# Encoder layer on one core: convolution results turned, and B·C scored, one projection later

## The chip, the cores and the metric

One core of a Trainium2 chip runs the whole layer in one launch. The metric is device time in microseconds (us), the median of three runs. The core has five engines that work side by side, each through its own list of instructions in the list's order: TensorE (PE, the matrix products), VectorE (DVE), ScalarE (ACT), GpSimd (POOL) and SyncE (SP, which here only sends transfers).

## What is computed

The reference is one layer of a bidirectional hybrid encoder: 512 positions, width 1024, float32. The change lies in branch A, a Mamba-2 SSD with 4 groups of 8 heads. Cut to that branch:

```
h = rms_norm(x)
z, xbc, dt_f, dt_b, q, k, v, gates = split_cols(h @ w_in, IN_SPLITS)
xbc = jax.nn.silu(depthwise_centred_conv(xbc, conv_w, conv_b))
xs, b_in, c_in = split_cols(xbc, (SSD_INNER, SSD_GROUPS * SSD_STATE, SSD_GROUPS * SSD_STATE))
...
cb = jnp.einsum('bclgn,bcsgn->bclsg', c_c, b_c)
y_diag = jnp.einsum('bclsg,bclsgr,bcsgrp->bclgrp', cb, decay, x_c)
states = jnp.einsum('bclgn,bclgr,bclgrp->bcgrpn', b_c, to_end, x_c)
y_off = jnp.einsum('bclgn,bcgrpn,bclgr->bclgrp', c_c, h_in, jnp.exp(a_cum).astype(dtype))
```

Forward and backward scans are added, gated with silu(z), normalised per group and projected back. Windowed attention, cross attention and a feed-forward part follow; they are not touched.

## The kernel before, in words

**Tiles.** The activations stand with their 1024 features in 8 slabs of 128 partitions by 512 positions. A weight tile `raw` (128 x 1024) is loaded by SP, split into a high part `whi` by ACT (L130) and a low part `wlo` by DVE (L131). One *projection* is 24 matmuls of 512 columns, three for each of 8 slabs (L140, L141, L142), into one of three PSUM banks named `mm`. A bank comes free when its last reader is through, and the projection three further on waits for that.

**A group.** For each of the 4 groups `group_in(g)` makes six projections: B, C and x0 to x3. `conv` then smooths each along the positions: ACT reads the bank (L412), DVE adds four shifted copies (L415, the last of which frees the bank), ACT takes a tanh into `cvt` (L417), DVE joins it to the result `bf`, `cf` or `xs` (L418). Three kinds of steps read these results on PE: `b_turn` transposes B (L433, four transposes, then a copy to `bt` on ACT, L434), `c_turn` multiplies B and C (L449, four matmuls, copy to `cb` on ACT, L450), and `x_turn(i)` transposes x(i) (L471, copy to `xk` on ACT, L472). Each step stands in the program behind a later projection, so that PE has that one to work on while the convolution is finished by DVE and ACT.

**What uses them.** `group_scan` has a list per head: SP loads rows of decay `rt` (three buffers), POOL masks them (`head`, L538, two selects a head), ACT takes eight exponentials (L545), POOL adds both directions into `mt` (L551, which also frees the `rt` buffer for the head three further on), DVE multiplies by `cb` (`times`, L556), PE multiplies with `xk` (`inner`, L566). `weigh` (POOL, L496) and `carry` (PE L504, DVE L509 and L511) build the states `hin`, `arrive` (PE, L578) applies them, `gather` (DVE and POOL, L586 to L591) adds up `vv`, `gate` (L603) multiplies with z. `group_out` (L645 for the first group, then L648 on DVE and L649 on POOL with a single buffer `cvt`) projects the group before. In group 0 its place is taken by projections of the cross attention's keys (`xw`, L262 on DVE).

**What sets the order.** Everything up to about 540 us stands in one block, `tc.block(schedule_with_timeline_sim=True)`. A scheduler, not the source, decides in which order each engine there gets its instructions; the source order is what it starts from. The lists it makes are fixed at build time: each engine then runs its own in that order. Behind the block the source order holds.

Of the kernel before, what the change touches and what calls it, by code (L numbers as in the profile page):

```python
# [55 lines left out]
ZP = 2  # L56
# [10 lines left out]
def weave(a, b):  # L67

    key = [((i + 0.5) / len(a), 0, i) for i in range(len(a))] + [((i + 0.5) / len(b), 1, i) for i in range(len(b))]
    return [(a, b)[w][i] for _, w, i in sorted(key)]  # L70
# [3 lines left out]
def bidir_hybrid_layer(ctx: ExitStack, tc: tile.TileContext, io, dbg=None):  # L74
# [20 lines left out]
    def bank(tag):  # L95
        return ps.tile([P, 512], F32, tag=tag, name=tag, bufs={"mm": 3, "sa": 2, "sb": 3}[tag])
# [99 lines left out]
    steps = []  # L196
# [7 lines left out]
    def full(src):  # L204
        return (src, 1024)
# [201 lines left out]
    def conv(w, ct, dst):  # L407
        sp, hcw = st["sp"], st["hcw"]
        acc = proj(w, st["hh"], st["hl"])
        u = sp.tile([P, S], F32, tag="cvu", name="cvu", bufs=2)  # L410
        w5 = [hcw[:, 5 * ct + j:5 * ct + j + 1] for j in range(5)]
        nc.scalar.activation(u, acc, AF.Identity, bias=hcw[:, 120 + ct:121 + ct], scale=w5[2])  # L412
        for j, a, b in ((0, slice(0, S - 2), slice(2, S)), (1, slice(0, S - 1), slice(1, S)),
                        (3, slice(1, S), slice(0, S - 1)), (4, slice(2, S), slice(0, S - 2))):
            nc.vector.scalar_tensor_tensor(u[:, b], acc[:, a], w5[j], u[:, b], op0=ALU.mult, op1=ALU.add)  # L415
        th = sp.tile([P, S], F32, tag="cvt", name="cvt", bufs=1)
        nc.scalar.activation(th, u, AF.Tanh)  # L417
        nc.vector.scalar_tensor_tensor(dst, th, 1.0, u, op0=ALU.add, op1=ALU.mult)  # L418

    def group_in(g):  # L420
        gb = G_SSD + 10 * g

        def b_step(w):
            sp = st["sp"]
            bf = sp.tile([P, S], F32, tag="bf", name="bf")
            conv(w, 16 + g, bf)
            st["bf", g] = bf

        def b_turn():
            bt = st["sp"].tile([P, S], F32, tag="bt", name="bt")  # L430
            tp = bank("sb")
            for c in range(NCH):
                nc.tensor.transpose(tp[:, c * P:(c + 1) * P], st["bf", g][:, c * P:(c + 1) * P], ident)  # L433
            nc.scalar.copy(bt, tp)  # L434
            st["bt", g] = bt

        def c_step(w):
            sp = st["sp"]
            cf = sp.tile([P, S], F32, tag="cf", name="cf", bufs=2)
            conv(w, 20 + g, cf)  # L440
            b_turn()
            st["cf", g] = cf

        def c_turn():
            cb = st["sp"].tile([P, S], F32, tag="cb", name="cb", bufs=2)
            tp = bank("sb")
            for c in range(NCH):
                c_ = slice(c * P, (c + 1) * P)
                nc.tensor.matmul(tp[:, c_], st["bf", g][:, c_], st["cf", g][:, c_], start=True, stop=True)  # L449
            nc.scalar.copy(cb, tp)  # L450
            st["cb", g] = cb

        def x_step(i):
            def f(w):
                sp = st["sp"]
                if i == 0:
                    st["xk", g] = sp.tile([P, NCH, S], F32, tag="xk", name="xk", bufs=2)
                xs = sp.tile([P, S], F32, tag="xs", name="xs", bufs=XSB)
                conv(w, 4 * g + i, xs)
                st["xs", g, i] = xs  # L460
                if i == 0:
                    c_turn()
                else:
                    x_turn(i - 1)()
            return f

        def x_turn(i):
            def f():
                tp = bank("sb")
                for c in range(NCH):  # L470
                    nc.tensor.transpose(tp[:, c * P:(c + 1) * P], st["xs", g, i][:, c * P:(c + 1) * P], ident)  # L471
                nc.scalar.copy(st["xk", g][:, :, i * P:(i + 1) * P], tp.rearrange("p (c l) -> p c l", c=NCH))  # L472
            return f

        w = io["w_in"]
        return ([(b_step, (full(w[gb]),)), (c_step, (full(w[gb + 1]),))]
                + [(x_step(i), (full(w[gb + 2 + i]),)) for i in range(4)], [(x_turn(3), ())])

    def group_z(g):
        def z_step(i):  # L480
            def f(w):
                acc = proj(w, st["hh"], st["hl"])
                zs = st["sp"].tile([P, S], F32, tag="zs", name="zs", bufs=4)
                nc.scalar.activation(zs, acc, AF.Tanh, scale=0.5)
                nc.vector.scalar_tensor_tensor(zs, zs, 1.0, acc, op0=ALU.add, op1=ALU.mult)
                st["zs", g, i] = zs
            return f
        return [(z_step(i), (full(io["w_in"][G_SSD + 10 * g + 6 + i]),)) for i in range(4)]
# [148 lines left out]
    def group_out(g):  # L637
        def f2(q):
            def f(w):
                for j in range(2):  # L640
                    m = 2 * q + j
                    acc = bank("mm")
                    mac(acc, w, st["vh"], st["vl"], nk=4, w0=4 * j)
                    if g == 0:
                        nc.vector.tensor_tensor(bs[:, m], acc, st["vrow"], op=ALU.mult)  # L645
                    else:
                        t = st["sp"].tile([P, S], F32, tag="cvt", name="cvt", bufs=1)
                        nc.vector.tensor_tensor(t, acc, st["vrow"], op=ALU.mult)  # L648
                        nc.gpsimd.tensor_tensor(bs[:, m], bs[:, m], t, op=ALU.add)  # L649
            return f  # L650
        return [(f2(q), (full(io["w_bs"][g, q]),)) for q in range(4)]


    def early_gate(m):
        def f(w):
            if m == 0:
                st["eg"] = st["sp"].tile([P, NCH, S], F32, tag="xk", name="xk", bufs=2)
            acc = proj(w, st["hh"], st["hl"])
            nc.scalar.activation(st["eg"][:, m], acc, AF.Tanh, scale=0.5)
        return f  # L660
# [10 lines left out]

    add(ssd_open)
    first, last = group_in(0)
    add(dt_step, full(io["w_in"][G_DT]))
    steps += weave(first, kv[KV0:KV1])
    for g in range(G):
        z, (more, turn) = group_z(g), group_in(g + 1) if g + 1 < G else ([], [])
        scan1, scan2 = group_scan(g)
        out = group_out(g - 1) if g else kv[KV1:]
        early = [(early_gate(m), (full(io["w_in"][G_GS + m]),)) for m in range(4)] if g == G - 1 else []  # L680
        kinds = {"m": list(more), "z": z[ZP:], "o": list(out), "e": early,
                 "r": [(group_rms, ())] if g else [], "w": [(group_row, ())] if g else []}

        def take(order):
            return [kinds[c].pop(0) for c in order if kinds[c]]

        one = take(ONE if g < G - 1 else ONE + "e")
        if g == 0:
            one += take("o" * len(kinds["o"]))
        two = take(TWO if g < G - 1 else LAST)  # L690
        steps += z[:ZP] + last
        steps += weave(scan1, one)
        steps += weave(scan2, two)
        last = turn
# [442 lines left out]
    for i, (fn, gr) in enumerate(steps):  # L1137
# [5 lines left out]
        w = ready[taken:taken + len(gr)]  # L1143
# [98 lines left out]
```

## Time and profile before

| quantity | value |
|---|---|
| median of 3 runs | 1304.64 us (1303.63 to 1304.96) |
| the profiled execution | 1304.59 us |
| its span, first to last instruction | 1302.8 us |
| outside the span | 1.8 us |
| PE busy | 1253.3 us |
| DVE, ACT, POOL busy | 770.9, 565.7, 314.8 us |

The profiled execution differs from the median by 0.05 us, so that its rows can be added and taken away as they stand. Times in the rows are counted from the start of the span. A bracket behind a row gives the idle time of the engine ahead of it and what ended it. PEclk is the share of full speed that TensorE's clock was granted: 1.0 is 2.4 GHz, 0.5 is 1.2 GHz.

### The profile page before, as it was taken

Reading aid. Unit: us, or ns where it says so; the run is one execution under the profiler, and the core shown is the slowest. Engines: PE = TensorE matmul, PEld = TensorE weight load, DVE = VectorE, ACT = ScalarE, POOL = GpSimd, SP = SyncE. Lnnn points to the kernel's source line nnn. Section 1 sums busy time; section 2 is a strip of 40 time slices with the busy share of each in tenths; the row PEclk is TensorE's granted clock in tenths of the full one; section 3 lists DMA queues with packets and bytes.
Section 4 is the critical chain, followed back from the end, with each engine's and each line's share of the span. In section 5 each row is a group of like instructions: output and inputs, shape, how many; then the busy total and the mean of one; then the engine's idle time right before and its main releaser. Section 6 shows DMA issues by size and latency. Waiting matters only on the chain.

```text
span 1302.8 us, 16247 instructions
## 1 busy us (share of the span) xinstructions
PE 1253.3 (96%) x6076; PEld 1015.5 (78%) x6076; DVE 770.9 (59%) x1226; ACT 565.7 (43%) x1062; POOL 314.8 (24%) x259
## 2 busy tenths in 40 slices
PE   7898999999989999999999999999999999999996
PEld 5677787778778688877667888887888888888886
DVE  6693987687787865678874345675444444432323
ACT  6456655365465232358783234444332222222220
POOL 2343742432671733211000002001111111110001
PEclk9899999999999999999999999999999999999998
DMA  7337563444354232331104233311322222233331
GB/s 267 121 112 196 158 202 113 130 146 140 105 157 133 81 116 79 120 97 33 49 29 139 95 104 108 125 65 65 97 90 98 95 96 98 95 93 101 93 98 65
DMA packets 49614, 143.48 MB, mean 110 GB/s; under 512 B 5120, under 2 KB 8576, under 8 KB 49536
## 3 DMA queue, kind: packets, MB, share of 16 engines
q1 hardware_dynamic: 47536, 138.58, 34.4%
q0 software_dynamic: 704, 2.10, 0.4%
q10 hardware_dynamic: 1296, 1.77, 0.4%
q8 instruction: 48, 0.79, 0.3%
q14 instruction: 30, 0.25, 0.1%
HBM read 137.97 MB, written 4.46 MB: 109 GB/s over the span
## 4 chain that ended last, share of the span: by engine, by line
PE 59%; issue 5%; DVE 2%; ACT 2%; POOL 1%; DVEq 0%; ACTq 0%; POOLq 0%
PE mm L140 18%; PE mm L141 18%; PE mm L142 18%; PE sb L824 1%; PE sb L811 1%; PE sb L998 1%; PE sa L967 1%; POOL rsw L723 1%; PE sa L783 1%; ACT rsw L722 0%; PE sa L785 0%; ACT whi L130 0%; ACT sm L796 0%; PE sb L155 0%; PE sb L173 0%
## 5 line engine op out<-in xcount | busy, mean ns | idle before, releaser
L130 ACT CAST whi<-raw 128x1024 fp32r<-128x1024 f32 (+2 forms) x192 | 198.8, 1036 | 457.5 <-PE mm L141 392.0
L140 PE MATMUL mm<-hh,whi 128*128 128x512 f32 x968 | 381.8, 395 | 8.1 <-ACT hh L316 4.7
L141 PE MATMUL mm<-hl,whi 128*128 128x512 f32 x968 | 381.0, 394 | 0.8 <-DVE hl L317 0.8
L142 PE MATMUL mm<-hh,wlo 128*128 128x512 f32 x968 | 381.0, 394 | 0.0
L131 DVE TENSOR_TENSOR wlo<-raw,whi 128x1024 fp32r<-128x1024 f32 (+2 forms) x193 | 238.1, 1234 | 143.6 <-ACT whi L130 134.2
L140 PEld LDWEIGHTS mm<-hh,whi 128*128 128x128 f32 x968 | 182.3, 189 | 47.9 <-ACT hh L316 4.9
L142 PEld LDWEIGHTS mm<-hh,wlo 128*128 128x128 f32 x968 | 182.6, 189 | 38.8 <-issue 2.2
L141 PEld LDWEIGHTS mm<-hl,whi 128*128 128x128 f32 x968 | 182.6, 189 | 37.6 <-issue 1.2
L545 ACT ACTIVATE rt<-rt,nb 128x128 f32<-128x128 f32 x256 | 78.6, 390 | 58.5 <-POOL rt L538 58.4
L188 POOL TENSOR_TENSOR sq_acc<-sq_acc,sq 128x512 f32<-128x512 f32 x14 | 24.4, 1741 | 261.0 <-ACT sq L187 261.0
L1051 POOL TENSOR_TENSOR fa<-fa,row 128x512 f32<-128x512 f32 x22 | 38.8, 1762 | 192.7 <-ACT fa L1050 192.7
L140 PE MATMUL mm<-vh,whi 128*128 128x512 f32 (+1 forms) x192 | 71.9, 375 | 6.9 <-DVE cvu L415 2.7
L415 DVE SCALAR_TENSOR_TENSOR cvu<-mm,hcw,cvu 128x510 f32<-128x510 f32 (+1 forms) x96 | 71.3, 743 | 7.0 <-ACT cvu L412 5.5
L140 PE MATMUL mm<-fh,whi 128*128 128x512 f32 (+1 forms) x198 | 72.7, 367 | 0.0
L141 PE MATMUL mm<-fl,whi 128*128 128x512 f32 (+1 forms) x198 | 72.4, 366 | 0.0
L142 PE MATMUL mm<-fh,wlo 128*128 128x512 f32 (+1 forms) x198 | 72.4, 366 | 0.0
L142 PE MATMUL mm<-vh,wlo 128*128 128x512 f32 (+1 forms) x192 | 71.8, 374 | 0.0
L141 PE MATMUL mm<-vl,whi 128*128 128x512 f32 (+1 forms) x192 | 70.3, 366 | 0.0
L538 POOL TENSOR_SCALAR_AFFINE_SELECT rt<-rt 128x512 f32<-128x512 f32 x64 | 49.7, 802 | 59.1 <-DMA rt<-adr 58.9
L1053 DVE TENSOR_TENSOR ft<-fa,mm 128x512 f32<-128x512 f32 x22 | 15.1, 688 | 73.6 <-PE mm L142 71.4
L551 POOL TENSOR_TENSOR mt<-rt 128x512 f32<-128x512 f32 x32 | 45.6, 1436 | 19.6 <-PE sa L566 19.5
L141 PE MATMUL mm<-ol,whi 128*128 128x512 f32 x128 | 50.0, 391 | 0.0
(231 smaller groups left out, 1963.5 us busy)
## 6 DMA issues: line engine op xcount, KB each, us to landing
raw<-in_w_in SPq DMA_DIRECT2D x69, 512.0 KB, 3.5
raw<-in_w_fi SPq DMA_DIRECT2D x44, 512.0 KB, 3.4
rt<-adr SPq DMA_DIRECT2D x32, 512.0 KB, 5.5
ear<-edr SPq DMA_DIRECT2D x32, 256.0 KB, 4.4
raw<-in_w_bs SPq DMA_DIRECT2D x16, 512.0 KB, 3.5
raw<-in_w_fo SPq DMA_DIRECT2D x16, 512.0 KB, 3.6
raw<-in_w_xk SPq DMA_DIRECT2D x8, 512.0 KB, 3.9
raw<-in_w_ba SPq DMA_DIRECT2D x8, 512.0 KB, 3.4
```

The lines of the kernel that those rows point to most:

```text
L130: nc.scalar.copy(hi[:, t], raw[:, t])
L131: (nc.gpsimd if i in LO_POOL else nc.vector).tensor_tensor(lo[:, t], raw[:, t], hi[:, t].bitcast(F32), op=ALU.subtract)
L140: nc.tensor.matmul(acc, wh, xh[:, k0 + k], start=first and k == 0, stop=False)
L141: nc.tensor.matmul(acc, wh, xl[:, k0 + k], start=False, stop=False)
L142: nc.tensor.matmul(acc, wl, xh[:, k0 + k], start=False, stop=last and k == nk - 1)
L188: eng.tensor_tensor(acc, acc, sq, op=ALU.add)
L415: nc.vector.scalar_tensor_tensor(u[:, b], acc[:, a], w5[j], u[:, b], op0=ALU.mult, op1=ALU.add)
L538: nc.gpsimd.affine_select(out=rt[:, d].rearrange("p (c l) -> p c l", c=NCH), in_=rt[:, d].rearrange("p (c l) -> p c l", c=NCH), pattern=[[ ...
L545: nc.scalar.activation(r, r, AF.Exp, bias=st["nb"][:, c, e0:e0 + 1])
L551: nc.gpsimd.tensor_tensor(mt, st["rt", g, h][:, 0], st["rt", g, h][:, 1], op=ALU.add)
L1051: nc.gpsimd.tensor_tensor(a, a, st["row2"], op=ALU.mult)
L1053: nc.vector.tensor_tensor(t, a, st["fp", 2 * j + 1], op=ALU.mult)
```

## The change

`b_turn` leaves `c_step` and stands behind x0's projection; `c_turn` moves from x0's to x1's; `x_turn(i)` from behind x(i+1) to behind x(i+2). So x2 and x3 are still to be turned when the six projections of a group are through: `x_turn(2)` now stands behind the first of the group's z projections and `x_turn(3)` behind the second, where `x_turn(3)` alone stood behind both.

```
         def c_step(w):
...
             conv(w, 20 + g, cf)
-            b_turn()
             st["cf", g] = cf
...
                 if i == 0:
+                    b_turn()
+                if i == 1:
                     c_turn()
-                else:
-                    x_turn(i - 1)()
+                elif i > 1:
+                    x_turn(i - 2)()
             return f
...
-                + [(x_step(i), (full(w[gb + 2 + i]),)) for i in range(4)], [(x_turn(3), ())])
+                + [(x_step(i), (full(w[gb + 2 + i]),)) for i in range(4)], [(x_turn(2), ()), (x_turn(3), ())])
...
-        steps += z[:ZP] + last
+        steps += z[:1] + last[:1] + z[1:ZP] + last[1:]
```

No instruction is added or left out. Since the scheduler starts from another list, the order within the block moves on every engine, for steps too that the diff doesn't name. Line numbers behind L460 are one higher in the changed kernel (L471 is L472 there), and the number behind a name counts tiles, so that the same tile can have another number.

**DVE, group 0, where x3 (`xs`, L418) is joined.** L556 is the product of a head's `mt` with `cb`, L131 a weight's low part, L485 a z projection. Before:

```order
L131 TENSOR_TENSOR wlo_919<-raw_916,whi_918 128x1024
L485 SCALAR_TENSOR_TENSOR zs_913<-zs_913,mm_888 128x512
L556 TENSOR_TENSOR mt_1213<-mt_1213,cb_666 128x512
L418 SCALAR_TENSOR_TENSOR xs_841<-cvt_873,cvu_867 128x512
L131 TENSOR_TENSOR wlo_965<-raw_962,whi_964 128x1024
```

and changed:

```order
L131 TENSOR_TENSOR wlo_919<-raw_916,whi_918 128x1024
L486 SCALAR_TENSOR_TENSOR zs_907<-zs_907,mm_882 128x512
L557 TENSOR_TENSOR mt_1206<-mt_1206,cb_741 128x512
L418 SCALAR_TENSOR_TENSOR xs_835<-cvt_867,cvu_861 128x512
L131 TENSOR_TENSOR wlo_965<-raw_962,whi_964 128x1024
```

Here nothing moved: x3's L418 stands behind the same product.

**DVE, between group 0 and group 1**, where L262 reads the keys' projection `mm_1023` and so frees the bank for x0 of group 1. `hin` are the states (L509, L511), `vv` is the sum that `gather` starts (L586). Before:

```order
L509 TENSOR_TENSOR hin0_1063<-hin0_1053,dec_174 128x512
L415 SCALAR_TENSOR_TENSOR cvu_1131<-mm_1106,hcw_414,cvu_1131 128x511
L262 TENSOR_TENSOR xw_1048<-mm_1023,sq_263 128x256
L131 TENSOR_TENSOR wlo_1234<-raw_1231,whi_1233 128x1024
L509 TENSOR_TENSOR hin1_1068<-hin1_1058,dec_174 128x512
L586 SCALAR_TENSOR_TENSOR vv_1472<-xs_713,vec_76,sa_1418 128x512
L511 TENSOR_TENSOR hin0_1063<-hin0_1063,sb_1061 128x512
```

and changed:

```order
L510 TENSOR_TENSOR hin0_1063<-hin0_1053,dec_174 128x512
L415 SCALAR_TENSOR_TENSOR cvu_1131<-mm_1106,hcw_414,cvu_1131 128x511
L587 SCALAR_TENSOR_TENSOR vv_1465<-xs_706,vec_76,sa_1411 128x512
L131 TENSOR_TENSOR wlo_1227<-raw_1224,whi_1226 128x1024
L510 TENSOR_TENSOR hin1_1068<-hin1_1058,dec_174 128x512
L262 TENSOR_TENSOR xw_1048<-mm_1023,sq_263 128x256
L512 TENSOR_TENSOR hin0_1063<-hin0_1063,sb_1061 128x512
```

The same L262 moved behind `vv`, a weight's low part and one L509.

**ACT, between group 2 and group 3**, where L417 takes the tanh for x0 of group 3. The `rt` rows are the exponentials of group 3's heads 1, 2 and 3. Before:

```order
L417 ACTIVATE cvt_3093<-cvu_3087 128x512
L130 CAST whi_3187<-raw_3185 128x1024
L545 ACTIVATE rt_3654<-rt_3654,nb_172 128x128 x8
L545 ACTIVATE rt_3666<-rt_3666,nb_172 128x128 x8
L187 ACTIVATE sq_3395<-vv_3224 128x512
```

and changed:

```order
L449 COPY cb_3271<-sb_3272 128x512
L546 ACTIVATE rt_3654<-rt_3654,nb_172 128x128 x8
L130 CAST whi_3180<-raw_3178 128x1024
L417 ACTIVATE cvt_3086<-cvu_3080 128x512
L546 ACTIVATE rt_3666<-rt_3666,nb_172 128x128 x8
```

The tanh and the weight's high part moved from ahead of head 2's exponentials to behind them.

**POOL, at the same place.** L649 adds a tile of the group before's output to `x1` and frees `cvt`; `rt_3680` is the row of head 4, `rt_3654` that of head 2. Before:

```order
L538 AFFINE_SELECT rt_3666<-rt_3666 128x512 x2
L591 TENSOR_TENSOR vv_3224<-vv_3224,ear_2971 128x384
L551 TENSOR_TENSOR mt_3730<-rt_3652 128x512
L649 TENSOR_TENSOR x1_69<-x1_69,cvt_3144 128x512
L649 TENSOR_TENSOR x1_69<-x1_69,cvt_3160 128x512
L188 TENSOR_TENSOR sq_acc_3232<-sq_acc_3232,sq_3395 128x512
L649 TENSOR_TENSOR x1_69<-x1_69,cvt_3204 128x512
L538 AFFINE_SELECT rt_3680<-rt_3680 128x512 x2
L551 TENSOR_TENSOR mt_3748<-rt_3654 128x512
```

and changed:

```order
L539 AFFINE_SELECT rt_3666<-rt_3666 128x512 x2
L552 TENSOR_TENSOR mt_3730<-rt_3652 128x512
L552 TENSOR_TENSOR mt_3748<-rt_3654 128x512
L539 AFFINE_SELECT rt_3680<-rt_3680 128x512 x2
L650 TENSOR_TENSOR x1_69<-x1_69,cvt_3137 128x512
L539 AFFINE_SELECT rt_3736<-rt_3736 128x512 x2
L650 TENSOR_TENSOR x1_69<-x1_69,cvt_3153 128x512
```

The adds of the output tiles moved from ahead of the selects of head 4 to behind them.

## Rows read from the trace of the kernel before

**Rows 1.** First part of the page: busy time, share, instructions of each engine

```profile
PE 1253.3 (96%) x6076; PEld 1015.5 (78%) x6076; DVE 770.9 (59%) x1226; ACT 565.7 (43%) x1062; POOL 314.8 (24%) x259
```

**Rows 2.** Waits of PE, 60 to 580 us: waiter, releaser, total us, times, longest

```profile
PE sb L471 <- DVE xs L418: 5.6, 3, 4.0
...
PE sa L382 <- DVE x L375: 2.4, 1, 2.4
```

**Rows 3.** Timeline of PE, 120 to 128 us: start, duration, instruction, idle ahead

```profile
122.44 0.63 PE L471 MATMUL sb<-cst,xs 128*128 128x128 f32 x4 [4.03 <-DVE xs L418]
```

**Rows 4.** Timeline of POOL, 104 to 124 us

```profile
118.08 1.22 POOL L538 TENSOR_SCALAR_AFFINE_SELECT rt<-rt 128x512 f32<-128x512 f32 x2 [5.77 <-DMA rt<-adr]
119.26 1.26 POOL L551 TENSOR_TENSOR mt<-rt 128x512 f32<-128x512 f32 x1
```

**Rows 5.** Timeline of DVE, 104 to 124 us

```profile
121.17 1.12 DVE L418 SCALAR_TENSOR_TENSOR xs<-cvt,cvu 128x512 f32<-128x512 f32 x1
```

**Rows 6.** Timeline of PE, 143 to 151 us

```profile
148.60 0.50 PE L140 MATMUL mm<-hh,whi 128*128 128x512 f32 x1 [1.30 <-DVE xw L262]
```

**Rows 7.** Timeline of DVE, 143 to 152 us

```profile
148.14 0.41 DVE L262 TENSOR_TENSOR xw<-mm,sq 128x256 f32<-128x256 f32 x1
148.47 1.67 DVE L131 TENSOR_TENSOR wlo<-raw,whi 128x1024 fp32r<-128x1024 f32 x1
...
151.75 0.67 DVE L511 TENSOR_TENSOR hin<-hin,sb 128x512 f32<-128x512 f32 x1
```

**Rows 8.** Timeline of PE around 188, 262 and 399 us

```profile
188.22 0.66 PE L471 MATMUL sb<-cst,xs 128*128 128x128 f32 x4 [1.00 <-DVE xs L418]
...
262.50 0.47 PE L140 MATMUL mm<-vh,whi 128*128 128x512 f32 x1 [1.83 <-DVE x L645]
...
399.36 0.63 PE L471 MATMUL sb<-cst,xs 128*128 128x128 f32 x4 [0.62 <-DVE xs L418]
```

**Rows 9.** Timeline of PE, 368 to 381 us

```profile
370.42 0.47 PE L140 MATMUL mm<-vh,whi 128*128 128x512 f32 x1 [2.68 <-DVE cvu L415]
...
373.27 0.60 PE L471 MATMUL sb<-cst,xs 128*128 128x128 f32 x4
...
376.92 1.05 PE L578 MATMUL sb<-cf,hin 128*128 128x128 f32 x8
...
379.63 0.50 PE L140 MATMUL mm<-hh,whi 128*128 128x512 f32 x1 [1.29 <-DVE cvt L648]
```

**Rows 10.** Timeline of ACT, 365 to 381 us

```profile
370.39 0.64 ACT L417 ACTIVATE cvt<-cvu 128x512 f32<-128x512 f32 x1 [4.26 <-DVE cvu L415]
370.93 1.04 ACT L130 CAST whi<-raw 128x1024 fp32r<-128x1024 f32 x1
371.87 4.79 ACT L545 ACTIVATE rt<-rt,nb 128x128 f32<-128x128 f32 x16
```

**Rows 11.** Timeline of DVE, 365 to 381 us

```profile
371.06 0.73 DVE L418 SCALAR_TENSOR_TENSOR xs<-cvt,cvu 128x512 f32<-128x512 f32 x1 [0.32 <-ACT cvt L417]
...
377.21 1.77 DVE L556 TENSOR_TENSOR mt<-mt,cb 128x512 f32<-128x512 f32 x1
378.90 0.68 DVE L648 TENSOR_TENSOR cvt<-mm,vrow 128x512 f32<-128x512 f32 x1
```

**Rows 12.** Timeline of POOL, 365 to 390 us

```profile
370.61 3.87 POOL L538 TENSOR_SCALAR_AFFINE_SELECT rt<-rt 128x512 f32<-128x512 f32 x4 [2.67 <-DMA rt<-adr]
...
379.65 1.30 POOL L649 TENSOR_TENSOR x<-x,cvt 128x512 f32<-128x512 f32 x1 [1.23 <-DVE cvt L648]
...
384.07 2.00 POOL L538 TENSOR_SCALAR_AFFINE_SELECT rt<-rt 128x512 f32<-128x512 f32 x2 [0.61 <-DMA rt<-adr]
```

**Rows 13.** Timeline of SP, 365 to 381 us: when a transfer is sent

```profile
377.62 0.37 SPq L519 DMA_DIRECT2D rt<-adr  x1
```

**Rows 14.** Windows: us, busy of PE, PEld, DVE, ACT, POOL, PEclk, DMA share, GB/s

```profile
123.60:127.00 3.40, 3.40 (x16) 3.21 (x15) 1.79 (x2) 2.06 (x5) 0.59 (x2) 0.50 0.70 213
...
370.00:374.00 4.00, 3.58 (x19) 3.05 (x20) 3.67 (x6) 3.61 (x10) 3.39 (x4) 1.00 0.22 86
```

## The prediction

> **What bounds the kernel now.** I read the page's first part, then PE's waits, then the timeline of PE at each of them, then the timelines of the engines that end them, beside the new order. PE is busy 1253.3 of 1302.8 us [rows 1], so about 50 us are idle, and the change can only touch the idle time that lies in the scheduled block. There the steps that it moves are waited for three times: L471 waits 5.6 us for DVE's L418, 4.0 of it once [rows 2]. That is the prize. What DVE, ACT and POOL do in between is not busy time that counts: they set the end only where PE stands idle for them.
>
> **The 4.03 us at 122.44 us stay.** This is the largest wait of a moved step, x3 of group 0 [rows 3]. It ends when DVE has done L418, started at 121.17 [rows 5]. The order on DVE shows that L418 stands behind a head's product L556, which needs POOL's L551, done at 120.52, which needs POOL's select at 118.08, and POOL had stood idle 5.77 us there for the transfer of the head's row [rows 4]. In the changed order the same product stands ahead of the same L418, and the transposes on PE are one matmul later. To come free of this wait, the transposes would have to be behind about 4 us more of PE's work, and they are not. Value: 0, bounds 0 and -4.03.
>
> **Where it gives.** In group 1, x0 and x1 are turned two projections later on PE: the 1.00 us at 188.22 goes; in group 3, x1's transposes move from 51.5 projections after the start of the block to 53, and the 0.62 us at 399.36 goes [rows 8]. Sum -1.6, bounds 0 and -1.6 (if what they waited for is late too). The 1.83 us at 262.50 [rows 8] ends with L645 of group 0's output, not with a moved step; I leave it. A moved step itself costs what it cost: four PE instructions and one ACT copy, no transfer.
>
> **Where it takes, first place, 148.60 us.** x0's projection of group 1 waits 1.30 us for L262 [rows 6], which DVE starts at 148.14 and finishes 0.05 us ahead of PE's start [rows 7]: no slack. In the new order three instructions that stood behind L262 stand ahead of it: L586, L131, L509. In the trace these three take from 148.47 to 151.75, 3.28 us [rows 7]. PE has two matmuls of `arrive` more to do meanwhile: L578 takes 1.05 us for eight such records, four matmuls [rows 9], hence about 0.5 us. So 3.28 - 0.5 = 2.8 us at the most; 0 if DVE, whose list there is also lighter further up, has run ahead. I take 2.0, nearer to the full price, since DVE's rows leave no gap in that stretch.
>
> **Second place, 370 to 380 us.** Before, ACT takes x0's tanh at 370.39 and a cast at 370.93, and only then 16 exponentials, 4.79 us [rows 10]; DVE joins x0 at 371.06 [rows 11] and PE turns it at 373.27 without a wait [rows 9]. In the new order the first eight exponentials and the cast stand ahead of the tanh, and the place of x0's transposes on PE is the same. The exponentials need POOL's select, which waited for a transfer until 370.61 [rows 12]; they can't be earlier than 371.87 unless the row is sent earlier, and the row's buffer is freed by an L551 that now stands behind an L649 (1.30 us [rows 12]).
> The least: 371.87 + 2.40 (half of 4.79) + 0.94 (from 370.93 to 371.87) = 375.2 for the tanh, 0.67 later (as from 370.39 to 371.06) DVE's L418 at 375.9, done at 376.6: PE turns x0 3.3 us later than at 373.27.
> The chain in full: the L649 in front makes the select 1.30 later, 371.9. DVE's new order has head 1's product (L556, 1.77 us [rows 11]) ahead of L418, and it needs an L551 that stands behind all four selects: 371.9 + 3.87 + 1.26 (L551 [rows 4]) = 377.0, + 1.77 + 0.73 = 379.5 for x0. Then POOL: L649 of the output's tiles stands behind head 4's select, where before it was done ahead of it. That select waits for a row sent at 377.62 [rows 13] and started at 384.07 [rows 12]; its buffer is freed by the L551 just computed, at about the same time, 377.0. So 384.07 + 2.00 (two selects) + 1.30 (L649) = 387.4, + 0.68 (L648 [rows 11]) = 388.1 for the bank that PE had at 379.63 [rows 9]. That is 8.5 us later. PE meanwhile does work that before came later: six matmuls of L578, by the row above some 1.5 us. Net 7.0.
> The bounds are 3.3 - 1.5 = 1.8 (only the tanh is late) and 7.0. I take 6.0, near the upper, since each instruction of the chain is named in the order and has a duration from a row. The waits that stand there now (2.68 and 1.29 [rows 9]) are inside these clock times and not counted again. What is late next is the chain of group 3's heads, which hangs on these same rows and so moves along.
>
> **The clock.** After the 4.03 us idle, TensorE ran 3.4 us at 0.50 [rows 14], the lower of its two levels, 1.2 GHz: it did in 3.4 us what takes 1.7 at 2.4 GHz. Such a fall follows three idles of PE in this stretch, of 2.4 us (L382 [rows 2]), 4.03 [rows 3] and 1.83 us [rows 8], three stretches of the same kind of which one row stands here; the 2.68 us at 370.42 was followed by full clock [rows 9, 14], and so was the 1.30 at 148.60. So an idle of 2 to 4 us costs 0 or 1.7 us more, and 3 of 5 rows say 1.7. New idles of that size: at 148.60 (1.30 + 2.0 = 3.3 us), ahead of x0's transposes and ahead of the output's bank (some 3 us each), and one more as the chain recovers. I take 1.0 for the first (3/5 of 1.7) and 2.6 for the others (one and a half falls); bounds 0 and 1.7, 0 and 5.1.
> The Trainium skill, "TensorE: Matmul & The Clock Gate", section "HAM oscillation — how this bites in real kernels", tells of a kernel whose clock fell to half in every wait between its bursts. Here the 2.68 us wait speaks against "every". [...]
>
> **The sum**, against the profiled execution of 1304.59 us (span 1302.8 and 1.8 around it; 0.05 under the median, so no correction): -1.6 + 2.0 + 1.0 + 6.0 + 2.6 = +10.0, hence 1314.6 us.
>
> **The rivals.**
> *Faster: the moved steps find their data.* If x3 of group 0 is no longer waited for, because POOL's select there starts earlier than at 118.08 (SP's list of rows changes too), the three waits of L471 go, 5.6 us, and with the longest the fall behind it, 1.7: 1304.6 - 7.3 = 1297.3. For it speaks that the moves are aimed at the right waits; against it that POOL's and DVE's order there is the same. It decides where that select ends over 4 us earlier, and none of the new waits may come. Chance 0.12.
> *Slower by more: every new wait brings the clock down.* The same places, with four falls: 1.7 + 5.1 in place of 1.0 + 2.6, so +13.2, 1317.8. For it: the falls after idles as short as 1.83 and 2.4; against it the 2.68. Chance 0.20.
> *No change: the new waits are absorbed.* DVE has run ahead at 148.60 (0), only the tanh is late at 373 (1.8), no fall, -1.6 gained: +0.2, 1304.8. For it: the heads' rows, not the moved steps, pace these stretches before and after, and the lists are the same in most places. Also in here is that the change hardly does what it says, since on PE the transposes of x0 in group 3 and of x3 in group 0 keep their places. Chance 0.15.
>
> **How the numbers follow.** The forecast has 0.53, the rivals 0.12, 0.20 and 0.15. Its own range is 1309 to 1317.5. The ends of all terms: -1.6 + 0 + 0 + 1.8 + 0 = +0.2 and -1.6 + 2.8 + 1.7 + 7.0 + 5.1 = +15.0, that is 1304.8 and 1319.6. From 1303 to 1320 all but the faster rival and the tails lie inside, so some 0.85. Within 0.2% is within 2.6 us, about what a measurement of this kernel can tell from no change. Faster 0.12, same 0.15, slower 0.53 + 0.20 = 0.73.
>
> **What would show it right or wrong.** Right: PE's waits list L262 with some 3 to 4 us and an L471 ahead of which PE idles 3 us or more near 375 us; the projection that started at 379.63 starts at 385 to 389; ACT shows eight L545 ahead of that tanh; PE's idle at 122 us is still about 4 us; the waits at 188 and 399 are gone. Wrong: PE busy from 370 to 390 with waits no longer than now, or the idle at 122 gone. It would also be wrong if a stretch that I left at nothing (240 to 300, 430 to 515 us) moved by over 2 us, since the order there hardly differs and I took its waits to move along.

## The result and the profile after

The changed kernel takes 1316.06 us (median of three runs) against 1304.8 us for the kernel before, run beside it. The ratio is 1.0089 with a 95% interval of 1.0068 to 1.0109, so it is slower by about 11.6 us (8.9 to 14.2). A fourth run, 1565.85 us at a mean granted clock of 0.75, was disturbed and stands outside these figures; with it the median is 1317.44 us. The profiled execution took 1318.83 us, its span is 1317.1 us: 14.3 us more than the span of before.

The first part of the page of the changed kernel (busy time, share and instructions of each engine) answers to [rows 1]:

```profile
PE 1259.1 (96%) x6076; PEld 1018.3 (77%) x6076; DVE 769.4 (58%) x1226; ACT 565.2 (43%) x1062; POOL 313.9 (24%) x259
```

The same 6076 matmuls keep PE busy for 5.8 us more (1259.1 against 1253.3), and PE is idle for 58.0 us of the span where it was 49.5, 8.5 us more. Equal work that takes longer is the clock (its mean is 0.983 where it was 0.989); the idle time is waits. So two fifths of the 14.3 us are clock, three fifths idle time. Part of that idle time lies at the start of this execution, ahead of any difference between the kernels. Counted from 60 us on (60 to 515 us of before, 63 to 529 of the changed kernel, the same work), PE's busy time grows from 432.5 to 438.7 us and its idle time from 22.3 to 27.4: 6.2 us of clock and 5.1 of waits. The waits of PE from 60 to 600 us in the changed kernel (waiter, releaser, total us, times, longest), which answer to [rows 2]:

```profile
PE sb L472 <- DVE xs L418: 6.4, 2, 3.4
PE mm L140 <- DVE cvu L415: 5.2, 4, 2.8
PE sa L567 <- DVE mt L557: 4.7, 5, 3.0
PE sb L579 <- ACT bt L434: 2.7, 1, 2.7
PE mm L140 <- DVE cvt L649: 2.5, 4, 1.4
```

The step that the change turns later (L472, L471 before) is waited for longer than before, 6.4 us for 5.6. L567's wait for the heads' products grows from 2.8 to 4.7 us and that for `cvu`, a convolution's sum, from 3.3 to 5.2. L579's wait for `bt`, the turned B, is new, and the wait for L262 that the prediction expected isn't there.

**Where the time went.** I set the same matmul of both traces side by side and took the difference of the starts. Counted by the time of before, the changed kernel is later by 2.9 us at 60, 2.2 at 138, 10.6 at 152, 7.9 at 190, 8.7 at 345, 15.8 at 380, 14.1 at 410, and 14.2 from there to the end. So 2.9 us are there before the lists of the two kernels differ at all, which begins near 100 us: that part is how this one execution started. The change's own share is 14.2 - 2.9 = 11.3 us, close to the 11.6 above. It gains 0.7 us up to 138, loses 6.4 in the first place (138 to 345, with the 1.00 us recovered at 188 in it) and 5.5 in the second (345 to 515).

These shares are those of one execution. Set beside the trace of before in the same way, other traces with the same lists there lose 3.1 to 5.7 us in the first place (experiments 1, 6 and 7 below) and 5.4 to 7.4 in the second (experiments 2 to 5). And experiment 2, which still has the lists of before there, is 1.9 us slower from 138 to 300. So a share read from one trace is good to about 2 us.

**First place.** PE's timeline in the changed kernel, 121 to 165 us (start, duration, instruction, idle ahead and what ended it), which answers to [rows 3] and [rows 6]:

```profile
124.80 0.63 PE L472 MATMUL sb<-cst,xs 128*128 128x128 f32 x4 [3.39 <-DVE xs L418]
...
130.48 0.50 PE L140 MATMUL mm<-hh,whi 128*128 128x512 f32 x1 [1.26 <-DVE zs L486]
...
147.66 1.97 PE L567 MATMUL sa<-mt,xk 128*64 128x128 f32 x14 [2.96 <-DVE mt L557]
...
157.21 1.22 PE L579 MATMUL sb<-cf,hin 128*128 128x128 f32 x4 [2.70 <-ACT bt L434]
158.08 0.77 PE L140 MATMUL mm<-hh,whi 128*128 128x512 f32 x1
```

The projection that waited for L262 in [rows 6] follows at 158.08 without a wait. DVE had finished L262 4 us earlier, in the changed kernel:

```profile
153.64 0.41 DVE L262 TENSOR_TENSOR xw<-mm,sq 128x256 f32<-128x256 f32 x1
```

What is late is `bt`. Followed backwards on ACT and POOL of the changed kernel (the same columns):

```profile
154.24 2.45 ACT L546 ACTIVATE rt<-rt,nb 128x128 f32<-128x128 f32 x8 [8.58 <-POOL rt L539]
156.60 0.56 ACT L434 COPY bt<-sb 128x512 f32<-128x512 f32 x1
```

```profile
151.86 2.94 POOL L539 TENSOR_SCALAR_AFFINE_SELECT rt<-rt 128x512 f32<-128x512 f32 x2 [6.06 <-DMA rt<-adr]
```

ACT copies `bt` behind eight exponentials, these wait 8.58 us for POOL's select, and that one 6.06 us for the transfer of a head's row `rt`. In the kernel before the same select waited 0.81 us for its row:

```profile
144.08 1.67 POOL L538 TENSOR_SCALAR_AFFINE_SELECT rt<-rt 128x512 f32<-128x512 f32 x2 [0.81 <-DMA rt<-adr]
```

SP's timeline shows why. First the kernel before, then the changed one, 130 to 150 us (start, time on SP, instruction; the third `raw<-in_w_xk` is the last of a set of three weight loads):

```profile
132.23 2.31 SPq L122 DMA_DIRECT2D raw<-in_w_xk  x2
138.18 0.38 SPq L519 DMA_DIRECT2D rt<-adr  x1
142.40 0.33 SPq L122 DMA_DIRECT2D raw<-in_w_xk  x1
```

```profile
135.56 9.69 SPq L122 DMA_DIRECT2D raw<-in_w_xk  x3
145.31 0.94 SPq L520 DMA_DIRECT2D rt<-adr  x2
```

Before, the row goes out at 138.18 and the third weight at 142.40. After, the third weight stands ahead of the row. It can't be sent before a `raw` buffer is free: from 130 to 150 us SP's weight loads wait 17.5 us in all for DVE's L131, which reads these buffers, against 10.0 before. SP sends in the order of its list, and so the row goes out at 145.31, 7.1 us later; 2.2 of these are the lateness that this execution already had at 138.

**Second place.** The changed kernel, 380 to 397 us. On POOL, then ACT, then DVE, then PE (the same columns; they answer to [rows 9 to 12], at times that are 8.7 us later from the first place on):

```profile
380.89 1.22 POOL L539 TENSOR_SCALAR_AFFINE_SELECT rt<-rt 128x512 f32<-128x512 f32 x2 [0.72 <-DMA rt<-adr]
383.51 1.22 POOL L539 TENSOR_SCALAR_AFFINE_SELECT rt<-rt 128x512 f32<-128x512 f32 x2 [1.40 <-DMA rt<-adr]
...
391.44 1.22 POOL L539 TENSOR_SCALAR_AFFINE_SELECT rt<-rt 128x512 f32<-128x512 f32 x2 [3.25 <-DMA rt<-adr]
```

```profile
381.56 2.45 ACT L546 ACTIVATE rt<-rt,nb 128x128 f32<-128x128 f32 x8 [5.34 <-POOL rt L539]
383.91 1.03 ACT L130 CAST whi<-raw 128x1024 fp32r<-128x1024 f32 x1
384.85 0.63 ACT L417 ACTIVATE cvt<-cvu 128x512 f32<-128x512 f32 x1
```

```profile
384.98 2.08 DVE L131 TENSOR_TENSOR wlo<-raw,whi 128x1024 fp32r<-128x1024 f32 x1 [2.88 <-ACT whi L130]
386.98 1.75 DVE L557 TENSOR_TENSOR mt<-mt,cb 128x512 f32<-128x512 f32 x1
388.66 0.68 DVE L418 SCALAR_TENSOR_TENSOR xs<-cvt,cvu 128x512 f32<-128x512 f32 x1
...
393.96 0.69 DVE L649 TENSOR_TENSOR cvt<-mm,vrow 128x512 f32<-128x512 f32 x1 [0.41 <-POOL x L650]
```

```profile
381.78 0.47 PE L140 MATMUL mm<-vh,whi 128*128 128x512 f32 x1 [2.83 <-DVE cvu L415]
...
389.39 1.12 PE L472 MATMUL sb<-cst,xs 128*128 128x128 f32 x4 [3.03 <-DVE xs L418]
...
395.52 0.39 PE L140 MATMUL mm<-hh,whi 128*128 128x512 f32 x1
```

This is the chain of the prediction: select, eight exponentials, cast, tanh, with the product L557 ahead of L418 on DVE. One link in it is not in the prediction: a weight's low part, L131, also stands ahead on DVE and waits 2.88 us for the cast behind the exponentials. PE waits 3.03 us for x0, which it had at once in [rows 9]. The output's bank, freed by the L649 at 393.96, is not waited for: the projection behind it starts at 395.52 without a gap.

**The clock.** Windows of the changed kernel behind these idles (us, busy of PE, PEld, DVE, ACT, POOL, PEclk, DMA share, GB/s), which answer to [rows 14]:

```profile
123.60:127.00 3.40, 2.20 (x15) 2.06 (x16) 1.05 (x2) 2.21 (x9) 1.46 (x2) 1.00 0.57 112
147.70:151.10 3.40, 3.40 (x16) 2.02 (x16) 3.40 (x6) 0.00 (x0) 0.00 (x0) 0.50 0.99 198
157.20:160.40 3.20, 3.19 (x10) 2.71 (x11) 1.92 (x4) 2.83 (x9) 2.24 (x3) 0.50 0.81 186
382.00:386.00 4.00, 4.00 (x12) 3.06 (x11) 1.12 (x2) 4.00 (x12) 2.60 (x5) 0.57 0.09 33
389.40:392.80 3.40, 3.40 (x17) 3.40 (x18) 1.70 (x3) 1.28 (x4) 1.36 (x3) 0.52 0.97 333
```

Of these five idles of PE of 2.7 to 3.4 us, four are followed by the lower level, 1.2 GHz; the longest, 3.39 us ahead of 124.80, is followed by 2.4 GHz.

What follows an idle differs from execution to execution. The wait of 2.83 us for `cvu` ahead of 381.78 stands in eight traces, those of the changed kernel and of experiments 2 to 7 and 9. In the 4 us behind it the granted clock is 0.50 to 0.63 in five of them and 1.00 in three (experiments 4, 6 and 9). The 2.96 us ahead of 147.66 are not even the change's own: experiment 2, with the lists of before there, waits 2.92 us at that matmul, and the full clock follows.

### The profile page after: what moved, and what is told of

The parts are those of the page before. It is cut to its first block, busy times and chain, and to the rows that moved or that the text cites. A ratio compares the mean times of both kernels' runs of the same rounds, so it can differ in the third digit from the quotient of the medians.

```text
span 1317.1 us, 16255 instructions
## 1 busy us (share of the span) xinstructions
PE 1259.1 (96%) x6076; PEld 1018.3 (77%) x6076; DVE 769.4 (58%) x1226; ACT 565.2 (43%) x1062; POOL 313.9 (24%) x259
## 4 chain that ended last, share of the span: by engine, by line
PE 74%; issue 7%; DMA 6%; DVE 5%; ACT 3%; POOL 3%; SPq 0%; POOLq 0%; ACTq 0%; DVEq 0%
PE mm L140 22%; PE mm L141 22%; PE mm L142 22%; DMA rt<-adr 4%; PE sb L825 1%; PE sb L579 1%; PE sb L812 1%; PE sb L505 1%; DVE wlo L131 1%; POOL rsw L724 1%; PE sb L999 1%; ACT whi L130 1%; ACT rt L546 1%; PE sa L968 1%; POOL rt L539 1%
## 5 line engine op out<-in xcount | busy, mean ns | idle before, releaser
L131 DVE TENSOR_TENSOR wlo<-raw,whi 128x1024 fp32r<-128x1024 f32 (+2 forms) x193 | 241.6, 1252 | 164.5 <-ACT whi L130 153.9
L539 POOL TENSOR_SCALAR_AFFINE_SELECT rt<-rt 128x512 f32<-128x512 f32 x64 | 46.6, 751 | 71.3 <-DMA rt<-adr 71.3
L140 PEld LDWEIGHTS mm<-vh,whi 128*128 128x128 f32 x192 | 37.2, 194 | 17.2 <-issue 5.1
```

Of the source, the lines that this page charges most:

```text
L131: (nc.gpsimd if i in LO_POOL else nc.vector).tensor_tensor(lo[:, t], raw[:, t], hi[:, t].bitcast(F32), op=ALU.subtract)
L140: nc.tensor.matmul(acc, wh, xh[:, k0 + k], start=first and k == 0, stop=False)
L539: nc.gpsimd.affine_select(out=rt[:, d].rearrange("p (c l) -> p c l", c=NCH), in_=rt[:, d].rearrange("p (c l) -> p c l", c=NCH), pattern=[[ ...
```

## The experiments

All of them need the lists held fast, since any edit of the source makes the scheduler draw new ones. So a table `ORDER` of instruction numbers is written into the kernel, one row an engine, and each instruction is tied to the one ahead of it in its row. This ties the order alone and adds no wait, and with the kernel's own numbers it gives the kernel's own lists. An experiment then exchanges entries.

```
+def pin(tc, nc):
+    at = {x.name: x for x in nc.cur_bb.bb.instructions}
+    for row in ORDER:
+        for a, b in zip(row, row[1:]):
+            tc.add_manual_dep(at[f"I-{b}"], f"I-{a}",
...
         if i == cutat:
+            pin(tc, nc)
             blk.close()
```

The table shifts the line numbers by 16 to 20: L579 is L596 or L599 there, L472 is L489 or L492, L262 is L279, L418 is L435 or L436.

**1 and 2: one part of the change each.** `LATE` names the groups whose turns stand later. For their part of the block the table has the lists of the changed kernel, for the rest those of the kernel before. Group 2's turns stand as before in both; in the changed kernel the stretch from 190 to 300 us, where they lie, loses nothing (7.9 us late, then 7.8).

```
+LATE = (0, 1)
...
+                if g not in LATE:
+                    (c_turn if i == 0 else x_turn(i - 1))()
...
+                else:
+                    (c_turn if i == 1 else x_turn(i - 2))()
```

> Only groups 0 and 1 have the later turns; a table of instruction numbers pins each engine's list in the block: as in the changed kernel up to the start of group 2, as in the kernel before from there on. Theory A (two separate losses, one between groups 0 and 1, one between groups 2 and 3, that add up): slower than before by 4 to 7 us, about 1310 us, with PE idle some 3 us ahead of L567 and some 2.7 us ahead of L579 between 147 and 158 us, and the waits of 370 and 379 us as before. Rival B (a delay early on is absorbed later, the loss is made at group 3): within 2 us of before.

> Only group 3 has the later turns; the lists are pinned as in the kernel before up to the middle of group 2 and as in the changed kernel from there on. Theory A: slower than before by 4 to 7 us, about 1310 us, with x0's transposes of group 3 waited for some 3 us. Rival B (the loss between groups 2 and 3 comes from being late already): within 2 us of before.

Groups 0 and 1 alone: 1308.97 us, ratio 1.0023 (1.0007 to 1.0038). Group 3 alone (`LATE = (3,)`): 1312.0 us, 1.005 (1.0031 to 1.0068). Against 1305.25 for before that is +3.7 and +6.75 (by the ratios 3.0 and 6.5), together 10.5, where the whole change costs 11.6. The first is a little less than expected. Each loss is there without the other, and within their intervals they add up: two places, neither the consequence of the other. PE of the first kernel shows the first place, with `bt`, and longer than in the whole change and than expected (5.55 us for 2.70):

```profile
154.22 1.22 PE L599 MATMUL sb<-cf,hin 128*128 128x128 f32 x4 [5.55 <-ACT bt L452]
```

**3, 4, 5: undo the exchange on SP, the one on DVE, both.** In the changed kernel's table, on SP:

```
-raw<-in_w_xk x3, rt<-adr x3
+raw<-in_w_xk x2, rt<-adr, raw<-in_w_xk, rt<-adr x2
```

and on DVE:

```
-L587 vv, L131 wlo, L510 hin, L262 xw
+L262 xw, L587 vv, L131 wlo, L510 hin
```

> The changed kernel, every list pinned as it is, with one exchange on SP: the row of head 6 of group 0 (rt) is sent ahead of one weight load (raw) instead of behind it, as it was before the change. Theory A (SP's queue makes the loss between groups 0 and 1: the row waits behind a load whose buffer is not free): 4 to 6 us faster than the changed kernel, about 1311 to 1312 us; the 2.7 us wait of L579 for bt goes. Rival B (the prediction's: L262 behind three more instructions on DVE): no change, 1316 to 1317 us.

> The changed kernel, every list pinned as it is, with L262 on DVE put back ahead of the three instructions (L587, L131, L510) that the change put in front of it. Rival B (the prediction's step): 2 to 4 us faster than the changed kernel. Theory A: no change, 1316 to 1317 us, since L262 is done in time for PE there.

> The changed kernel, pinned, with both exchanges at the first place: head 6's row sent ahead of the weight load (SP) and L262 ahead of the three instructions (DVE). With the row alone exchanged, PE still waited 2.0 us for L262. Theory A' (two limits one behind the other: the row first, L262 next): 1.5 to 3 us faster than with the row alone, so some 6 us faster than the changed kernel, 1310 to 1311.5 us, and no wait over 1.5 us for L262 or bt around 150 us. Rival (L262 is a limit of its own that never decides): as with the row alone, 1313 us.

Gains over the changed kernel are taken from the ratios. The row alone: 1313.17 us (1.0055, 1.0038 to 1.0072), some 4 us less than the changed kernel. L262 alone: 1317.15 us (1.0092, 1.0064 to 1.0119), no gain; its four runs lie between 1312.62 and 1319.01 us, so that one of 2 or 3 us could hide in them. Its trace says why none is to be expected: PE still waits for `bt`, and not for L262.

```profile
150.40 0.71 PE L596 MATMUL sb<-cf,hin 128*128 128x128 f32 x4 [3.35 <-ACT bt L451]
```

Both: 1311.38 us (1.0041, 1.0024 to 1.0059), 6 us less. PE with the row alone restored, 148 to 154 us:

```profile
149.56 0.71 PE L596 MATMUL sb<-cf,hin 128*128 128x128 f32 x4 [0.68 <-ACT bt L451]
152.27 0.50 PE L157 MATMUL mm<-hh,whi 128*128 128x512 f32 x1 [2.00 <-DVE xw L279]
```

With the row back in its place the wait for `bt` falls from 2.70 to 0.68 us, and L262 (L279 here), which had been hidden by it, is now waited for 2.00 us in all; the prediction had 1.30 + 2.0 = 3.3. With both restored that wait is gone too, and set beside the trace of before the kernel is 1.0 us late at 138 and 1.2 at 345: in this trace the first place costs next to nothing. The step from the row alone to both, 1.8 us by the ratios, is within the noise; it is the wait that vanishes which shows L262 as the second limit.

**6 and 7: the second place.** First on ACT alone, then on ACT, DVE (`xs` ahead of the product, a weight's low part and a sum) and POOL (two L650 ahead of the selects of head 4):

```
-rt x8, whi, cvt, rt x8
+cvt, whi, rt x16
```

```
-ear, wlo, mt, xs, mt
+xs, ear, wlo, mt x2
...
-AFFINE_SELECT x2, x, AFFINE_SELECT x2, x x3
+x x2, AFFINE_SELECT x4, x x2
```

> The changed kernel, pinned, with one exchange on ACT between groups 2 and 3: the cast of a weight's high part and x0's tanh stand ahead of head 2's eight exponentials, as before the change. Theory C (a chain on three engines: DVE's list has x0's L418 behind a head's product that needs POOL): under 1.5 us faster than the changed kernel, 1315 to 1317 us, and L472 still waited for over 2 us near 389 us. Rival (the tanh's place on ACT is the loss, the lower bound of the prediction): 2 to 4 us faster, 1312 to 1314 us.

> The changed kernel, pinned, with the order of three engines put back between groups 2 and 3: on ACT cast and tanh ahead of head 2's exponentials, on DVE x0's L418 right behind its last shifted copy, on POOL two adds of output tiles ahead of head 4's selects. Theory C: 4 to 6 us faster than the changed kernel, 1311 to 1312.5 us; the wait of L472 near 389 us goes. Rival (the loss there comes from the rows' transfers, whatever the order): under 2 us.

The tanh alone: 1316.68 us (1.0074, 1.0046 to 1.0102), which can't be told from the changed kernel. Three engines: 1312.66 us (1.005, 1.0033 to 1.0068), nearly 5 us less. With the tanh alone moved, ACT, DVE and PE show:

```profile
376.61 0.63 ACT L434 ACTIVATE cvt<-cvu 128x512 f32<-128x512 f32 x1 [5.64 <-DVE cvu L432]
```

```profile
381.78 1.74 DVE L574 TENSOR_TENSOR mt<-mt,cb 128x512 f32<-128x512 f32 x1 [2.35 <-POOL mt L569]
383.44 0.68 DVE L435 SCALAR_TENSOR_TENSOR xs<-cvt,cvu 128x512 f32<-128x512 f32 x1
```

```profile
384.27 1.09 PE L489 MATMUL sb<-cst,xs 128*128 128x128 f32 x4 [4.63 <-DVE xs L435]
```

The tanh is done at 377.24, yet x0 is joined at 383.44: DVE stands idle 2.35 us for the product's `mt`, with L418 (L435 here) ready behind it. The limit is DVE's list, not ACT's. With all three restored the wait for x0 is gone from PE, but a wait of 1.93 us for the output's bank appears in its place, at 386.14, and the 2.83 us for `cvu` stay. Beside the trace of before the second place then costs 2.8 us (4.6 late at 345, 7.4 at 515) in place of 5.5. Experiment 9 below has the same lists there, and its trace loses 5.8 us in this stretch, so how much of the second place these exchanges give back is not settled.

**8: the cause put into the kernel before.** No turn moves; only SP's exchange of experiment 3 is made, the other way round, in the table of before.

> The kernel before, pinned, with the one exchange on SP the other way: head 6's row of group 0 sent behind the weight load. Nothing else is changed, the turns stand where they stood. Theory A (the queue makes the loss, not the moved steps): slower than before by 3 to 5 us, 1308 to 1310 us. Rival (it takes the moved steps to lose there): within 1.5 us of before.

1311.29 us, 1.0036 (1.0021 to 1.0051): 4.7 us more than before by the ratio (2.7 to 6.7), 6.3 by the medians. The row goes out at 145.40 and POOL's select waits 7.98 us for it. PE loses its time later than in the changed kernel:

```profile
151.89 1.23 POOL L555 TENSOR_SCALAR_AFFINE_SELECT rt<-rt 128x512 f32<-128x512 f32 x2 [7.98 <-DMA rt<-adr]
```

```profile
167.11 0.94 PE L595 MATMUL sb<-cf,hin 128*128 128x128 f32 x6 [2.71 <-DVE ear L607]
...
196.47 0.99 PE L488 MATMUL sb<-cst,xs 128*128 128x128 f32 x4 [3.89 <-DVE xs L435]
```

One weight load ahead of one row costs at least as much as the first place did in experiment 1 (3.0 us by the ratio). Where PE feels it depends on the rest of the lists.

**9 and 10: is anything left of the moves themselves?** All exchanges of 5 and 7 in the changed kernel; and the exchanges of 5 in the kernel with `LATE = (0, 1)`.

> The changed kernel, pinned, with both places put back: head 6's row and L262 ahead at the first place, the order of ACT, DVE and POOL at the second. If the two losses are separate and these exchanges are what makes them: about 1306 to 1309 us, within 4 us of before, the rest being the waits of 2.8 us for a shifted copy that stay near 378 us. If they hang together otherwise: above 1310 us.

> Only groups 0 and 1 have the later turns, lists pinned, and at the first place head 6's row and L262 stand ahead as before. Theory D (the later turns themselves take the wait of 188 us away and cost nothing): 0 to 2 us faster than before, 1303 to 1305 us. Rival (the later turns cost by themselves, in late xk, bt and cb): 1 to 4 us slower, 1306 to 1309 us.

The first: 1308.7 us, 1.0025 (1.0007 to 1.0043), so some 3 us of the 11.6 remain. Its PE still waits 2.8 us for `cvu` and 3.3 for the output's bank in group 3; which list makes these wasn't singled out, and the lists of PE and SP, which differ there too, were not exchanged in any run. The second: 1305.31 us, 0.9994 (0.998 to 1.0009), the time of before. In groups 0 and 1 the later turns cost nothing of their own that can be told (the interval is 2 us either way), and the wait at 188 us that they remove (1.00 us, [rows 8]) isn't seen in the time either. Neither is faster than the kernel before.

**11 and 12: the change without the scheduler.** The table holds PE, ACT, DVE and POOL to the order of the source, once for each kernel; only SP's transfers are still placed by the scheduler.

> The kernel before with the lists of PE, DVE, ACT and POOL in the order in which the program is written; only SP's transfers are still placed by the scheduler. It stands here for the pair with the next run. Slower than before by some tens of us, since nothing is moved to fill waits; the x turns are waited for at many places.

> The changed kernel in the same way, in written order. Theory D (each turn has one projection, some 5.5 us, more to hide behind; the loss comes from what the scheduler made of the list): 5 us or more faster than the run in written order without the change, with less waiting of L472. Rival (the move is a loss in itself): the same or slower.

1407.41 us (1406.22 to 1413.24) and 1406.41 us (1404.98 to 1407.54): 1 us apart, with intervals that overlap (1.0747 to 1.0818, 1.0732 to 1.0801). The waits of PE from 60 to 600 us, in the order of the source of before, then of after:

```profile
PE sb L594 <- ACT cb L466: 7.7, 1, 7.7
PE sb L465 <- DVE cf L434: 7.6, 1, 7.6
...
PE mm L156 <- ACT whi L146: 4.7, 3, 1.9
...
PE sa L582 <- DVE mt L572: 1.1, 2, 0.7
```

```profile
PE sb L595 <- ACT bt L450: 7.5, 1, 7.5
...
PE mm L156 <- ACT whi L146: 6.5, 4, 3.0
...
PE sa L583 <- DVE mt L573: 2.9, 2, 1.8
```

Written out, the move does what it says: the waits for `cb` and for C, 15.3 us, are gone. In their place stands one for `bt` of 7.5 us, and other waits grow (`whi` from 4.7 to 6.5, `mt` from 1.1 to 2.9). Over the whole span PE is idle for 114.6 us where it was 120.8, and busy for 1289.3 where it was 1283.6. So the move takes 6.2 us of waits away, and the clock takes 5.7 back: its mean is 0.954 against 0.959 in the profiled executions, and 0.954 to 0.956 against 0.954 to 0.960 over all four runs of each. The gain in time of 5 us or more that was expected didn't come.

With intervals of some 4.6 us either way these two runs show no loss and no gain of the move itself, in a kernel that is 100 us slower. That the loss is the work of the lists that the scheduler drew is shown for the first place: in experiments 3, 5, 8 and 10 exchanged entries make it or take it away. For the second, experiments 6, 7 and 9 show the chain on DVE and give a part back; the 3 us that experiment 9 leaves stay without a cause.

## Why the prediction was right, and where it wasn't

**The sign and the size.** +10.0 us were forecast and 11.6 measured, halfway to the +13.2 of the rival "every new wait brings the clock down"; the times don't tell the two apart. The total hides errors that cancel. In the profiled execution the first place was put too low by some 4 us, the second too high by 2.5 (in the other traces 1 to 4 and 0.6 to 2.6). By kind, 6.4 us of waits were forecast and 5.1 measured from 60 us on, 3.6 of clock and 6.2. That the sum came out so near is in part luck.

**The wait at 122 us: right.** It is 3.39 us in place of 4.03 (2.77 to 5.30 in experiments 1, 3 to 7, 9 and 10), and the row ahead of it comes no earlier. A second wait, 1.26 us for `zs` at 130.48, takes the rest back; the full clock behind 124.80 gave the 0.7 us that the stretch gained.

**The gains: right.** The waits of [rows 8] at 188 and 399 are gone; that this is worth 1.6 us of time, no run shows.

**The first place: the step that failed.** The prediction put it at L262 on DVE ("three instructions that stood behind L262 stand ahead of it"), for 2.0 us and 1.0 of clock. With the 1.00 us gained at 188 that is +2.0 up to 345, and +3.5 by the upper bounds; it measured +6.4. Of these 1.7 are more idle time and 4.7 longer busy time; in the traces of experiments 6 and 7 the same lists lose 2.7 and 0.4, and 4.1 and 1.6. L262 is late in the changed list, as argued, but the row is later still: I walked through DVE's, ACT's and POOL's lists and not through SP's, where in this stretch one exchanged pair stands. The prediction has no term for that row. The mechanism that I priced is the second limit behind it: PE waits 2.00 us for it in experiment 3, where 3.3 were forecast, and it is without effect as long as the row is late (experiment 4). SP's list ended in no row of the prediction, though [rows 4] show POOL idle 5.77 us for such a row: how late a row may be sent was the question to ask of each of them.

**The second place: right in mechanism, too large in its second half.** +6.0, 2.6 of clock and -0.6 make 8.0; it measured 5.5 (5.4 to 7.4 in experiments 2 to 5). The first half hit: L418 was worked out to end at 379.5, that is 388.2 with the 8.7 us of the first place, and it ended at 389.3. Experiment 6 confirms that the product ahead of it on DVE decides, not the tanh. The second half was over-priced: the bank was put at 388.1, so 396.8, and was free at 394.7. Of the 2.1 us between, 1.3 are the row of head 4: its select was put at 384.07, so 392.8, and began at 391.44. The other 0.8 are the select itself, 1.22 us where [rows 12] had 2.00. The four selects taken at 3.87 us hold: from 380.89 to 384.73 they take 3.84, with a wait of 1.40 for the second row in between. And by then PE had lost its time elsewhere, at `cvu` and at x0, so that the bank was no limit.

**The clock: under-priced.** 3.6 us were taken, with 3 in 5 for a fall; from 60 us on PE's busy time grew by 6.2. The 3 in 5 came from a thin base: of its five idles only those of 2.4 and 2.68 us lie in the 2 to 4 us that it is said for, and they went one each way; the 1.81 us ahead of 144.28, followed by the full clock, was not counted. Four of the five idles in the windows above were followed by the lower level, which in this execution bears out the rival "every new wait brings the clock down" in this term better than the forecast. It isn't so in every execution: in the profiled one of experiment 4 PE is busy for 1253.3 us, as in the kernel before, though PE waits 2.83 and 4.59 us in the second place. The Trainium skill, "TensorE: Matmul & The Clock Gate", section "HAM oscillation — how this bites in real kernels", tells of waits of some 3 to 5 us, each followed by a cold start. Of the idles here two are as long as that: the trace agrees for the 3.03 us and not for the 3.39; and it has falls behind 2.70, 2.83 and 2.96.

**The stretches left at nothing** moved by under 2 us, as said: 240 to 300 gave back 0.9 us, and 430 to 515 moved by 0.8.

## What to carry to other kernels

When a scheduler draws the lists, price the lists and not the diff: compare every engine's list, SP's first, since one load that waits for its buffer holds up everything that is sent behind it. A named wait that vanishes in an experiment often uncovers the next limit, a few microseconds behind; undo suspects in pairs before calling one of them harmless. And split a loss into longer busy time for the same instructions and more idle time: the first is the clock, the second the waits.

## What else the runs showed

**The start of an execution varies.** With equal lists up to about 100 us, the changed kernel's profiled execution was 2.9 us late at 60 us, and those of experiments 5 and 7 were 1.6 late and 0.6 early. A difference of two traces should be counted from behind that stretch.

**The clock makes much of the noise.** Of 17 executions of the kernel before that ran beside experiments 1 to 4, the two fastest, 1302.68 and 1302.9 us, have a mean granted clock of 0.989 and 0.990; the slowest, 1309.91 us, has 0.984.

**POOL's selects can slow down beside DVE.** The same pair of selects takes 1.21 to 1.23 us in every case where DVE has nothing to do during both, and up to 2.95 us (2.94 at 151.86, above) where DVE is busy throughout. But a busy DVE does not always slow them: it is at work during nearly all of the pair at 380.89 in the changed kernel and throughout the pair at 151.89 in experiment 8, and they take 1.22 and 1.23. The Trainium skill, "Perfetto Trace Analysis", section "Optimizing Scalar/DVE Operations", says that GpSimd and VectorE share a read port of SBUF. The slow pairs agree with that, the fast ones beside a busy DVE show that it is not all, and no run here separates the causes.
